# Inverse roots of two normalisations on one engine, and another order for the last step of the down projection

## The chip, the cores and the metric

The kernel runs on one core of a Trainium2 chip. The core has five engines, each with a queue of instructions that it works through in order: TensorE (PE, matrix products, its weight loads shown as PEld), VectorE (DVE), ScalarE (ACT), GpSimd (POOL) and SyncE (SP), which here only issues transfers. Transfers run on 16 DMA engines beside them. Engines wait for each other on semaphores. The metric is the time of one execution on the device in microseconds (us), the median of several runs.

## The reference

One block of a sequence model for 1024 positions of 1024 channels, in float32. What matters here is the second half: the attention output is projected and added to the residual, normalised, and a gated feed-forward layer follows; a last normalisation makes the output.

```python
def rmsnorm(x, g):
    xf = x.astype(jnp.float32)
    xf = xf * lax.rsqrt(jnp.mean(xf * xf, axis=-1, keepdims=True) + RMS_EPS)
    return (xf * g.astype(jnp.float32)).astype(x.dtype)
...
        merged = (jax.nn.sigmoid(gate_a) * y_a + jax.nn.sigmoid(gate_b) * y_b) @ w_o[l]
        x = x + g1 * merged

        h = modulate(rmsnorm(x, norm2_g[l]), sh2, sc2)
        ffn = (jax.nn.silu(h @ w_ffn_gate[l]) * (h @ w_ffn_up[l])) @ w_ffn_down[l]
        x = x + g2 * ffn
    return rmsnorm(x, norm_f_g)
```

## The kernel before, in words

Positions are cut into eight row blocks of 128 (t = 0 to 7), channels into halves of 512. Every matrix product in float32 precision is made of three products of split operands: a high part h (a cast on ScalarE), a low part l (the rest, a subtraction on VectorE), and the pairs (h,h), (h,l), (l,h). A scheduler moves instructions of the program within each engine's queue; the order that it chose is what the rows further down show.

**Attention output** (`attend_out`, lines 1112 to 1178). For every row block two PSUM tiles of 128x512 are made and added to x (line 1141). ScalarE squares the row and sums it (line 1150); `rstd` (lines 479 to 497) turns the sum into an inverse root; ScalarE multiplies (line 1152), TensorE transposes (line 1160), and the scaled transposes are the operands of the feed-forward layer.

`rstd` works on 128x1: VectorE scales and adds epsilon (line 485, and 487 where two half sums come), ScalarE takes Ln (488) and Exp(-0.5 x) (489), and VectorE corrects that by one Newton step: a = y v y (491), a = 1.5 - 0.5 a (495), y = y a (496).

**Down projection** (`down`, lines 1280 to 1412). It is a product of 1024 x 2816 by 2816 x 1024 after Strassen's scheme: blocks of half the rows by half the channels, and seven products (numbered 1 to 7) in place of eight. The 20 pairs of channels blocks that go this way are done in three steps of 4, 3 and 3 (`STEPS`); two last blocks come afterwards in plain form (`rest`). In each step the products run in `ORDER` = 2, 4, 5, 3, 1, 6, 7. For a product, sums of weight blocks are made on POOL (line 1339), cast on ScalarE (1340), the low part taken on VectorE (1341); then four PSUM tiles t of 128x512, each of 9 matmuls in a step of three (line 1356), are added by VectorE to that product's own accumulator `acc[i]` (line 1362). An accumulator is two buffers, each with two of the four tiles.

Four of the accumulators (4, 5, 7, 6) also hold the residual of their block and gather the result. What Strassen's scheme adds between them is done by POOL in the last step (`closing`, line 1317, table `CLOSE`): for each n, the position of a product in the step, a list of (target, source, operation), four tiles each. `closing(n)` stands in the program ahead of the matmul tiles of position n, and `closing(7)` behind the step.

PSUM has eight banks of 128x512, named gu (1), wo (3) and tq (4). `self.banks` hands them out in turn. Each product takes four, so a product has the banks of the one two positions ahead of it.

**Tail** (lines 1380 to 1412). For each row block in the order 4, 5, 6, 7, 0, 1, 2, 3 (`ROWS`) two tiles of six matmuls give the rest of the sum (line 1396). VectorE adds the gathered block (1398); ScalarE squares (1406; for the last row in halves, 1400); `close` calls `rstd`, multiplies by the root and the gain (1381; last row 1375 on ScalarE for the left half and 1376 on VectorE for the right) and sends the row out (1378, 1382). Rows 4 to 7 read accumulators 2 and 6, rows 0 to 3 accumulators 7 and 5.

Of the kernel before, what the change touches and what calls it, by code (L numbers as in the profile page):

```python
# [9 lines left out]
F32 = mybir.dt.float32  # L10
# [18 lines left out]
class S5:  # L29
# [270 lines left out]
    def run(self, m, u_src, y_dst, more):  # L300
# [56 lines left out]
        if more:  # L357
# [30 lines left out]
SIGN_A = {i: ALU.subtract if i in (6, 7) else ALU.add for i in range(1, 8)}  # L388
SIGN_B = {i: ALU.subtract if i in (3, 4) else ALU.add for i in range(1, 8)}

CLOSE = {2: ((6, 2, ALU.subtract),), 3: ((2, 4, ALU.add),), 4: ((7, 4, ALU.add),), 5: ((7, 5, ALU.subtract), (5, 3, ALU.add)),
         6: ((6, 3, ALU.add), (6, 1, ALU.add)), 7: ((7, 1, ALU.add),)}
SLOT = {3: 0, 6: 1, 7: 2, 4: 3, 1: 4, 2: 5, 5: 6}

AENG = {(i, 1) for i in range(1, 8)} | {(2, 0)}
# [32 lines left out]
class Block:  # L428
# [47 lines left out]
        (lo or nc.vector).tensor_tensor(l, a, h.bitcast(F32), ALU.subtract)  # L476
        return h, l

    def rstd(self, pool, ss, n, more=None, at=None):

        nc = self.nc
        v = at("v") if at else pool.tile([P, n], F32, name="rv")
        y = at("y") if at else pool.tile([P, n], F32, name="ry")
        a = at("a") if at else pool.tile([P, n], F32, name="ra")
        nc.vector.tensor_scalar(v, ss if more is None else more, 1.0 / 1024.0, 1e-6, ALU.mult, ALU.add)
        if more is not None:
            nc.vector.scalar_tensor_tensor(v, ss, 1.0 / 1024.0, v, ALU.mult, ALU.add)
        self.after(nc.scalar.activation(y, v, AF.Ln), self.fence)
        nc.scalar.activation(y, y, AF.Exp, scale=-0.5)
        if n == 1:  # L490
            nc.vector.scalar_tensor_tensor(a, y, v, y, ALU.mult, ALU.mult)
        else:
            nc.vector.tensor_tensor(a, y, y, ALU.mult)
            nc.vector.tensor_tensor(a, a, v, ALU.mult)
        nc.vector.tensor_scalar(a, a, -0.5, 1.5, ALU.mult, ALU.add)
        nc.vector.tensor_tensor(y, y, a, ALU.mult)
        return y

    def after(self, ins, first):
# [617 lines left out]
    def attend_out(self, mg, g1, const, tp, pp, tpp):  # L1117
# [5 lines left out]
        for c in range(2):  # L1123
# [7 lines left out]
            for t in range(KT):  # L1131
                if c or t > 3:
                    ps[t] = pp.tile([P, 512], F32, name="wo")
                    self.wo_product(ps[t], t, range(KT), mg, ws)
                elif t == 0:
                    for tt in range(4):
                        ps[tt] = tpp.tile([P, 512], F32, name="tq")
                    for k in range(KT):
                        for tt in range(4):
                            self.wo_product(ps[tt], tt, (k,), mg, ws)  # L1140
                nc.vector.tensor_tensor(x1[t][:, cs], ps[t], x1[t][:, cs], ALU.add)
                if c == 0:
                    continue
                nc.sync.dma_start(out=self.xD[P * t:P * t + P], in_=x1[t])
                if t % 4 == 0:
                    f = [[self.F.tile([P, 2, 512], F32, name=f"f{y}") for _ in range(2)] for y in range(2)]
                xh = self.rp.tile([P, 1024], F32, name="row") if t % 4 == 3 else tp.tile([P, 1024], F32, name="xh")
                xhs.append(xh)
                ss = const.tile([P, 1], F32, name="ss2", bufs=2)
                nc.scalar.activation(xh, x1[t], AF.Square, accum_out=ss)  # L1150
                r = self.rstd(const, ss, 1)
                nc.scalar.mul(xh, x1[t], r)
                if t % 2 == 0:
                    continue
                for k in range(0, KT, 2):
                    q = tpp.tile([P, 512], F32, name="tq").rearrange("p (k t) -> p k t", k=2)
                    s = slice(P * (t % 4 - 1), P * (t % 4 - 1) + 256)
                    for kk in range(2):
                        for tt in range(2):
                            nc.tensor.transpose(q[:, kk, P * tt:P * tt + P], xhs[t - 1 + tt][:, P * (k + kk):P * (k + kk) + P], self.ident)  # L1160
                        o = f[k // 4][k % 4 // 2][:, kk, s]
                        G_, m_ = G[:, k + kk:k + kk + 1], mod[:, k + kk:k + kk + 1]
                        if kk:
                            nc.vector.tensor_scalar(o, q[:, kk], G_, m_, ALU.mult, ALU.add)  # L1164
                        else:
                            nc.scalar.activation(o, q[:, kk], AF.Identity, bias=m_, scale=G_)
                if t == 3:
                    b11, b21 = f
                    self.B = {2: self.pieces(2, b11, None, self.PA, "pa"), 4: self.pieces(4, b21, b11, self.PA, "pa")}
# [111 lines left out]
    def down(self, const, tp, g2, gf):  # L1281
# [38 lines left out]
        last_sum = None  # L1320
        stages = Turns(*[(self.W, "wb", 4)] * 4, *self.stages.pools)
        for s, np_ in enumerate(STEPS):
            W = [(weights(2 * p), weights(2 * p + 1)) for p in range(p0, p0 + np_)]
            if s == len(STEPS) - 1:
                WL = [weights(20 + m) for m in range(2)]
            for n, i in enumerate(ORDER):
                ops = []
                (ay, ax), b = TERMS_B[i]
                for p in range(np_):
# [10 lines left out]
                        nc.scalar.copy(h, st)  # L1340
                        nc.vector.tensor_tensor(l, st, h.bitcast(F32), ALU.subtract)
                    ops.append((h, l))
                if s == len(STEPS) - 1:
                    if n == 6:
                        rest = []
                        for m in range(2):
# [4 lines left out]
                for t in range(4):  # L1351
# [7 lines left out]
                    if s == 0 and i not in FROM:  # L1359
                        (nc.scalar.copy if (n * 4 + t) % 2 else nc.vector.tensor_copy)(m[i], ps)  # L1360
                    else:
                        nc.vector.tensor_tensor(m[i], ps, m[i], ALU.add)
            p0 += np_
        closing(7)
        ops = rest
        out = self.out.rearrange("o (t p) d -> p (o t) d", p=P)
        L, R = slice(0, 512), slice(512, 1024)

        def at(t):
            return lambda n: small[:, t, "vya".index(n) + 2:"vya".index(n) + 3]  # L1370

        def close(t, row, ss):
            if t == ROWS[-1]:
                r = self.rstd(const, ss[:, 1:2], 1, ss[:, 0:1], at(t))
                nc.scalar.mul(row[:, L], row[:, L], r)
                nc.vector.scalar_tensor_tensor(row[:, R], row[:, R], r, gf[:, R], ALU.mult, ALU.mult)
                for cs in (L, R):
                    nc.sync.dma_start(out=out[:, t, cs], in_=row[:, cs])
                return
            r = self.rstd(const, ss[:, 0:1], 1, None, at(t))  # L1380
            nc.vector.scalar_tensor_tensor(row, row, r, gf, ALU.mult, ALU.mult)
            nc.sync.dma_start(out=out[:, t], in_=row)

        small = const.tile([P, KT, 5], F32, name="ss3")
        last = None
        for t in ROWS:
            ss = small[:, t, 0:2]
# [2 lines left out]
            for c in range(2):  # L1390
# [8 lines left out]
                if t == ROWS[-1]:  # L1399
                    nc.scalar.activation(sq[:, cs], row[:, cs], AF.Square, accum_out=ss[:, c:c + 1])  # L1400
                    if c == 0:
                        nc.gpsimd.tensor_tensor(row[:, cs], row[:, cs], gf[:, cs], ALU.mult)
                if c == 0 and last:
                    close(*last)
# [136 lines left out]
```

## Time and profile before

| What | Value |
|---|---|
| runs | 1508.24, 1510.94, 1508.77 us |
| median | 1508.77 us |
| the profiled execution's own time | 1510.83 us |
| its span | 1509.1 us |
| mean granted TensorE clock | 0.974 |
| HBM read, written | 142.40 MB, 48.76 MB |

The span goes from the first to the last instruction of the execution that was profiled, and its own time is a little longer than the span. Times in the trace are microseconds from the span's start. Names are the program's: `tq`, `wo`, `gu` are PSUM banks, `pb` and `x1` (shown as `x` by the profile) the buffers of the accumulators, `pa` the rows of weights and of the output, `ss` the small sums. "out<-in" gives what is written and what is read; a name in square brackets behind a row is the instruction that ended the idle time before it.

In the last stage the span divides so: step 2's products end near 1410, the last step runs to about 1468, the rest rows to 1493, and behind them no matmul stands.

### The profile page before, as it was taken

What the parts mean: (1) busy time and instruction counts of PE and PEld (TensorE: products, weight loads), DVE (VectorE), ACT (ScalarE), POOL (GpSimd) and SP (SyncE); (2) the same over time, 40 slices, a digit from 0 to 9 for tenths busy, and PEclk for the clock granted to TensorE, in tenths of its full rate; (3) what the DMA queues carried; (4) which work ended last, traced back from release to release, by engine and by line L of the source; (5) the groups of instructions that cost most, each with busy time, mean ns of one, the idle gap of its engine ahead of it and who ended that gap; (6) DMA issues with size and microseconds to landing.
All of it is one profiled execution on the core that took longest, in us unless ns stands there. A gap on an engine that the chain in (4) does not pass through costs nothing.

```text
span 1509.1 us, 18300 instructions
## 1 busy us (share of the span) xinstructions
PE 1421.0 (94%) x6706; PEld 1121.5 (74%) x6706; DVE 1137.7 (75%) x1523; ACT 582.8 (39%) x764; POOL 610.9 (40%) x306
## 2 busy tenths in 40 slices
PE   5898999999999999999799799999999998999995
PEld 3678888787666666668688588888888886888774
DVE  5879995457897888868526886666666669999997
ACT  3321122722565655663226533333333334433323
POOL 1000000102555555414300235444444468788795
PEclk9999999999999999999899899999999999999998
DMA  9555665489011112136422233333333346455312
GB/s 341 136 108 165 165 159 150 130 272 328 15 49 49 37 34 77 56 104 217 175 84 106 76 125 113 105 105 105 106 105 105 104 154 235 136 161 176 102 49 112
DMA packets 180410, 193.55 MB, mean 128 GB/s; under 512 B 28636, under 2 KB 130080, under 8 KB 180320
## 3 DMA queue, kind: packets, MB, share of 16 engines
q1 hardware_dynamic: 171184, 184.86, 38.9%
q10 hardware_dynamic: 8912, 7.48, 1.8%
q8 instruction: 53, 0.87, 0.2%
q14 instruction: 37, 0.30, 0.1%
q0 software_dynamic: 224, 0.05, 0.0%
HBM read 142.40 MB, written 48.76 MB: 127 GB/s over the span
## 4 chain that ended last, share of the span: by engine, by line
PE 51%; DVE 20%; issue 10%; POOL 9%; DMA 5%; ACT 4%; SPq 1%; DVEq 0%; POOLq 0%; ACTq 0%
PE tq L1257 10%; PE wo L1257 8%; PE ga L735 4%; PE wo L1114 4%; PE mm L735 3%; PE mm L809 3%; PE gu L1257 3%; PE mx L809 3%; POOL ws L874 3%; PE mm L643 2%; PE mx L735 2%; PE tq L1114 2%; PE acc L809 1%; POOL pb L1317 1%; PE z L809 1%
## 5 line engine op out<-in xcount | busy, mean ns | idle before, releaser
L874 POOL TENSOR_SCALAR ws<-wa 128x1024 f32<-128x1024 f32 (+1 forms) x40 | 108.5, 2712 | 112.9 <-DVE wa L871 59.2
L473 POOL TENSOR_TENSOR ws<-wb 128x1024 f32<-128x1024 f32 x26 | 64.2, 2471 | 193.8 <-DVE f L1164 90.9
L457 POOL TENSOR_TENSOR wl<-ws,wh 128x1024 fp32r<-128x1024 f32 x12 | 28.9, 2410 | 127.0 <-ACT wh L454 127.0
L294 POOL MEMSET tz<- 128x1024 f32 x4 | 3.8, 954 | 178.0 <-PE mm L643 95.9
L877 DVE TENSOR_TENSOR ws<-wa,ws 128x1024 f32<-128x1024 f32 (+1 forms) x40 | 46.6, 1165 | 35.5 <-ACT ws L876 35.1
L875 ACT ACTIVATE ws<-ws 128x1024 f32<-128x1024 f32 (+1 forms) x40 | 38.8, 971 | 74.7 <-POOL ws L874 74.7
L1310 POOL TENSOR_TENSOR pa<-pa,row 128x1024 f32<-128x1024 f32 x22 | 64.7, 2965 | 1.8 <-DMA pa<-in_w_ffn_down_dram 1.6
L473 POOL TENSOR_TENSOR wgs<-wb 128x1024 f32<-128x1024 f32 x14 | 34.6, 2473 | 72.3 <-DVE wgl L476 30.9
L1248 POOL TENSOR_TENSOR f<-f,f 128x512 f32<-128x512 f32 x30 | 50.0, 1692 | 26.9 <-DVE f L1238 18.3
L879 DVE TENSOR_TENSOR wl<-ws,wh 128x1024 fp32r<-128x1024 f32 (+1 forms) x40 | 55.2, 1381 | 1.1
L902 DVE TENSOR_TENSOR wa<-wa,acc 128x512 f32<-128x512 f32 (+1 forms) x80 | 46.7, 623 | 2.1 <-PE acc L809 1.8
L454 ACT CAST wh<-ws 128x1024 fp32r<-128x1024 f32 x24 | 25.1, 1048 | 59.9 <-PE wo L1114 36.3
L979 DVE SCALAR_TENSOR_TENSOR acc<-aw,cond,acc 128x512 f32<-128x512 f32 x56 | 43.8, 781 | 5.9 <-DMA aw<-in_w_ada_dram 5.1
L1237 ACT ACTIVATE f<-f 128x1024 f32<-128x1024 f32 x22 | 23.4, 1061 | 62.7 <-DVE f L1277 32.8
L1339 POOL TENSOR_TENSOR wb<-pa 128x512 f32<-128x512 f32 x23 | 40.6, 1776 | 15.6 <-DVE wxl L1337 5.5
L809 PE MATMUL z<-q,k 64*128 64x512 f32 (+3 forms) x192 | 41.8, 526 | 3.8 <-DVE wa L871 2.6
L1248 POOL TENSOR_TENSOR f<-f 128x512 f32<-128x512 f32 x20 | 42.2, 2129 | 0.0
L905 ACT ACTIVATE wa<-wa 128x1024 f32<-128x1024 f32 (+1 forms) x40 | 38.5, 963 | 9.0 <-DVE wa L902 9.0
L1356 PE MATMUL wo<-f,f 128*128 128x512 f32 x132 | 40.6, 389 | 0.0
L809 PE MATMUL mm<-wa,V 128*64 128x512 f32 (+3 forms) x192 | 39.8, 507 | 0.0
L900 ACT CAST row<-acc 1x1024 fp32r<-1x1024 f32 (+2 forms) x32 | 27.0, 842 | 31.2 <-PE acc L809 31.0
L876 ACT ACTIVATE ws<-ws 128x1024 f32<-128x1024 f32 (+1 forms) x40 | 38.6, 966 | 0.5
(844 smaller groups left out, 4725.0 us busy)
## 6 DMA issues: line engine op xcount, KB each, us to landing
aw<-in_w_ada_dram SPq DMA_DIRECT2D x64, 256.0 KB, 4.4
hD<-f SPq DMA_DIRECT2D x30, 512.0 KB, 2.9
ws<-in_w_in_dram SPq DMA_DIRECT2D x23, 512.0 KB, 4.6
wb<-in_w_ffn_gate_dram SPq DMA_DIRECT2D x44, 256.0 KB, 4.1
wb<-in_w_ffn_up_dram SPq DMA_DIRECT2D x44, 256.0 KB, 4.3
pa<-in_w_ffn_down_dram SPq DMA_DIRECT2D x22, 512.0 KB, 4.6
wb<-hD SPq DMA_DIRECT2D x40, 256.0 KB, 2.8
x<-in_x_dram SPq DMA_DIRECT2D x16, 512.0 KB, 6.9
```

Source lines behind the costliest of these rows:

```text
L473: (add or nc.gpsimd).tensor_tensor(st, a, b, op)
L735: self.nc.tensor.matmul(ps, lhsT=w[a][:, k], rhs=act[h][k][:, b], start=(j == 0), stop=(j == n - 1))
L809: return self.tc.keep_in_program_order(self.nc.tensor.matmul(*args, **kw))
L874: nc.gpsimd.tensor_scalar(st, a, EXACT, None, ALU.min)
L877: nc.vector.tensor_tensor(st, a, st, ALU.max)
L879: nc.vector.tensor_tensor(lt, st, ht.bitcast(F32), ALU.subtract)
L902: nc.vector.tensor_tensor(a[:, x, 0:f], a[:, x, 0:f], r[:, x, 0:f], ALU.subtract)
L979: nc.vector.scalar_tensor_tensor(acc, w[:, j], cj, acc, ALU.mult, ALU.add)
L1114: self.nc.tensor.matmul(ps, lhsT=mg[t // 4][k][:, a, P * (t % 4):P * (t % 4) + P], rhs=ws[k // 2][b][:, k % 2], start=k + j == 0, stop=k + ...
L1248: nc.gpsimd.tensor_tensor(o, a, b, op)
L1257: self.nc.tensor.matmul(ps, lhsT=w[x][:, q, k], rhs=self.B[i](y, k), start=(j == 0), stop=(j == 11))
L1310: nc.gpsimd.tensor_tensor(w, w, g2, ALU.mult)
```

## The change

Three things are changed.

1. `rstd` keeps its old form for another place only. At the attention output and at the end, `rstd_s` takes its place: six operations on ScalarE. With s the sum of squares: y = exp(-0.5 ln(s/1024 + eps)), h = -0.5 (s/1024 + eps), h = h y, h = h y + 1.5, y = y h. Epsilon and 1.5 come from a small buffer `eps` that POOL fills with three stores at the start. For the last row, two more operations of ScalarE turn the first half's sum into the addends for the second half's.

2. In the last step the products run in the order 5, 2, 4, 1, 3, 6, 7 (`LAST`), and `CLOSE` is rewritten for it; nothing is closed behind the step.

3. In the last step products 3 and 1 are no longer added to their own accumulators but to the two blocks that they belong to each (`DIRECT`): 3 to blocks 5 and 6, 1 to blocks 6 and 7. The parts of products 3 and 1 from the earlier steps still come through POOL's closings. There are 32 closing additions of 128x512 before and after, and eight more additions of VectorE after.

```diff
-CLOSE = {2: ((6, 2, ALU.subtract),), 3: ((2, 4, ALU.add),), 4: ((7, 4, ALU.add),), 5: ((7, 5, ALU.subtract), (5, 3, ALU.add)),
-         6: ((6, 3, ALU.add), (6, 1, ALU.add)), 7: ((7, 1, ALU.add),)}
+LAST = (5, 2, 4, 1, 3, 6, 7)
+CLOSE = {1: ((7, 5, ALU.subtract),), 2: ((5, 3, ALU.add), (6, 3, ALU.add)), 3: ((6, 2, ALU.subtract), (6, 1, ALU.add)),
+         4: ((7, 1, ALU.add), (2, 4, ALU.add)), 5: ((7, 4, ALU.add),)}
+DIRECT = {3: (5, 6), 1: (6, 7)}
...
+    def rstd_s(self, ss, y, h, b=None):
+
+        act = self.nc.scalar.activation
+        b, bh = b or (self.eps[:, 0:1], self.eps[:, 1:2])
+        self.after(act(y, ss, AF.Ln, bias=b, scale=1.0 / 1024.0), self.fence)
+        act(y, y, AF.Exp, scale=-0.5)
+        act(h, ss, AF.Identity, bias=bh, scale=-0.5 / 1024.0)
+        self.nc.scalar.mul(h, h, y)
+        act(h, h, AF.Identity, bias=self.eps[:, 2:3], scale=y)
+        self.nc.scalar.mul(y, y, h)
         return y
...
+        self.eps = const.tile([P, 3], F32, name="eps")
+        for n, x in enumerate((1e-6, -0.5e-6, 1.5)):
+            nc.gpsimd.memset(self.eps[:, n:n + 1], x)
...
-                r = self.rstd(const, ss, 1)
+                r = self.rstd_s(ss, *(const.tile([P, 1], F32, name=n, bufs=2) for n in ("r2", "h2")))
...
+            final = s == len(STEPS) - 1
...
-            for n, i in enumerate(ORDER):
+            for n, i in enumerate(LAST if final else ORDER):
...
-                        nc.vector.tensor_tensor(m[i], ps, m[i], ALU.add)
+                        for z in DIRECT.get(i, (i,)) if final else (i,):
+                            nc.vector.tensor_tensor(m[z], ps, m[z], ALU.add)
             p0 += np_
-        closing(7)
...
             if t == ROWS[-1]:
-                r = self.rstd(const, ss[:, 1:2], 1, ss[:, 0:1], at(t))
+                r = self.rstd_s(ss[:, 1:2], small[:, t, 2:3], small[:, t, 3:4], (small[:, t, 4:5], small[:, t, 5:6]))
...
-            r = self.rstd(const, ss[:, 0:1], 1, None, at(t))
+            r = self.rstd_s(ss[:, 0:1], small[:, t, 2:3], small[:, t, 3:4])
...
                     if c == 0:
+                        for n, f in ((4, 1.0), (5, -0.5)):
+                            nc.scalar.activation(small[:, t, n:n + 1], ss[:, 0:1], AF.Identity, bias=self.eps[:, n - 4:n - 3], scale=f / 1024.0)
                         nc.gpsimd.tensor_tensor(row[:, cs], row[:, cs], gf[:, cs], ALU.mult)
```

Behind the lines of the diff the queues of the engines look as follows at three places. Lines of the changed kernel are some ten higher than those of before: its closings are line 1327, VectorE's adds from PSUM 1374, the low parts 1352, the weight sums 1350.

POOL in the last step, before. The buffers are the accumulators: pb_9843/44 is 4, pb_9847/48 is 5, pb_9851/52 is 7, x1_9855/56 is 2, x1_9857/58 is 3, x1_9859/60 is 1 and x1_9861/62 is 6.

```order
L1317 TENSOR_TENSOR pb_9851<-pb_9851,pb_9847 128x512 x2
L1317 TENSOR_TENSOR pb_9852<-pb_9852,pb_9848 128x512 x2
L1317 TENSOR_TENSOR pb_9847<-pb_9847,x1_9857 128x512 x2
L1317 TENSOR_TENSOR pb_9848<-pb_9848,x1_9858 128x512 x2
L1317 TENSOR_TENSOR x1_9861<-x1_9861,x1_9857 128x512 x2
L1317 TENSOR_TENSOR x1_9861<-x1_9861,x1_9859 128x512
L1317 TENSOR_TENSOR x1_9862<-x1_9862,x1_9858 128x512
L1317 TENSOR_TENSOR x1_9861<-x1_9861,x1_9859 128x512
L1317 TENSOR_TENSOR x1_9862<-x1_9862,x1_9858 128x512
L1317 TENSOR_TENSOR x1_9862<-x1_9862,x1_9860 128x512
L1317 TENSOR_TENSOR pb_9851<-pb_9851,x1_9859 128x512
L1317 TENSOR_TENSOR x1_9862<-x1_9862,x1_9860 128x512
```

POOL in the last step of the change. Here 4 is pb_9839/40, 5 is pb_9843/44, 7 is pb_9847/48, 2 is x1_9851/52, 3 is x1_9853/54, 1 is x1_9855/56 and 6 is x1_9857/58.

```order
L1327 TENSOR_TENSOR pb_9844<-pb_9844,x1_9854 128x512
L1327 TENSOR_TENSOR x1_9858<-x1_9858,x1_9852 128x512
L1350 TENSOR_TENSOR ws_11424<-pa_10967 128x512
L1327 TENSOR_TENSOR x1_9858<-x1_9858,x1_9852 128x512
L1350 TENSOR_TENSOR ws_11431<-pa_10973 128x512
L1327 TENSOR_TENSOR x1_9857<-x1_9857,x1_9855 128x512
L1350 TENSOR_TENSOR wgs_11438<-pa_10979 128x512
L1327 TENSOR_TENSOR x1_9857<-x1_9857,x1_9855 128x512
L1327 TENSOR_TENSOR x1_9851<-x1_9851,pb_9839 128x512 x2
L1327 TENSOR_TENSOR x1_9858<-x1_9858,x1_9856 128x512
L1327 TENSOR_TENSOR x1_9852<-x1_9852,pb_9840 128x512
L1327 TENSOR_TENSOR x1_9858<-x1_9858,x1_9856 128x512
```

Before, the additions to block 6 are among POOL's last work of the step. In the change they stand between weight sums (line 1350) for the last two products, and the last row here is the 31st from the first addition to block 6 in this step, `x1_9857<-x1_9857,x1_9853`.

VectorE at products 3 and 1 of the last step, before: each tile goes to its own accumulator.

```order
L1341 TENSOR_TENSOR wl_11345<-wb_11342,wh_11344 128x1024
L1362 TENSOR_TENSOR x1_9857<-gu_11222,x1_9857 128x512
L1362 TENSOR_TENSOR x1_9857<-wo_11233,x1_9857 128x512
L1362 TENSOR_TENSOR x1_9858<-wo_11244,x1_9858 128x512
L1341 TENSOR_TENSOR wgl_11352<-wb_11349,wgh_11351 128x1024
L1362 TENSOR_TENSOR x1_9858<-wo_11255,x1_9858 128x512
L1341 TENSOR_TENSOR wxl_11411<-ws_11408,wxh_11410 128x1024
L1341 TENSOR_TENSOR f0_11418<-ws_11415,f0_11417 128x1024
L1362 TENSOR_TENSOR x1_9859<-tq_11291,x1_9859 128x512
L1362 TENSOR_TENSOR x1_9859<-tq_11302,x1_9859 128x512
L1362 TENSOR_TENSOR x1_9860<-tq_11313,x1_9860 128x512
L1341 TENSOR_TENSOR f0_11425<-wgs_11422,f0_11424 128x1024
```

VectorE at products 1 and 3 of the change.

```order
L1374 TENSOR_TENSOR pb_9847<-gu_11230,pb_9847 128x512
L1374 TENSOR_TENSOR x1_9857<-wo_11242,x1_9857 128x512
L1374 TENSOR_TENSOR pb_9847<-wo_11242,pb_9847 128x512
L1352 TENSOR_TENSOR wgl_11372<-wb_11369,wgh_11371 128x1024
L1352 TENSOR_TENSOR wxl_11427<-ws_11424,wxh_11426 128x1024
L1352 TENSOR_TENSOR f0_11434<-ws_11431,f0_11433 128x1024
L1374 TENSOR_TENSOR pb_9843<-tq_11307,pb_9843 128x512
L1374 TENSOR_TENSOR x1_9857<-tq_11307,x1_9857 128x512
L1374 TENSOR_TENSOR x1_9858<-wo_11254,x1_9858 128x512
L1374 TENSOR_TENSOR pb_9848<-wo_11254,pb_9848 128x512
L1374 TENSOR_TENSOR pb_9843<-tq_11319,pb_9843 128x512
L1374 TENSOR_TENSOR x1_9857<-tq_11319,x1_9857 128x512
```

Tiles of the banks wo and tq now go to block 6 (x1_9857/58) and to another block each, and the low parts for products 6 and 7 (line 1352) stand between them in the queue.

ScalarE at the very end, before: the two half squares of the last row, and Ln and Exp of the last two rows.

```order
L1400 ACTIVATE ft_11688,ss3_11505<-pa_11687 128x512
L488 ACTIVATE ss3_11505<-ss3_11505 128x1
L1400 ACTIVATE ft_11688,ss3_11505<-pa_11687 128x512
L489 ACTIVATE ss3_11505<-ss3_11505 128x1
L488 ACTIVATE ss3_11505<-ss3_11505 128x1
L489 ACTIVATE ss3_11505<-ss3_11505 128x1
L1375 ACTIVATE pa_11687<-pa_11687,ss3_11505 128x512
```

ScalarE at the very end of the change, from the last half square on.

```order
L1408 ACTIVATE ft_11692,ss3_11509<-pa_11691 128x512
L499 ACTIVATE ss3_11509<-ss3_11509 128x1
L498 ACTIVATE ss3_11509<-ss3_11509 128x1
L500 ACTIVATE ss3_11509<-ss3_11509 128x1
L501 ACTIVATE ss3_11509<-ss3_11509 128x1
L499 ACTIVATE ss3_11509<-ss3_11509 128x1
L502 ACTIVATE ss3_11509<-ss3_11509,eps_91 128x1
L501 ACTIVATE ss3_11509<-ss3_11509 128x1
L503 ACTIVATE ss3_11509<-ss3_11509 128x1
L502 ACTIVATE ss3_11509<-ss3_11509,eps_91 128x1
L503 ACTIVATE ss3_11509<-ss3_11509 128x1
L1383 ACTIVATE pa_11691<-pa_11691,ss3_11509 128x512
```

Ten operations of 128x1 now stand between the last half square and the product; no other engine works between them.

More of the change, by code (lines that the diff above doesn't have):

```diff
@@ L477, in operand, with rstd @@
         return h, l
-    def rstd(self, pool, ss, n, more=None, at=None):
+    def rstd(self, pool, ss, n):
         nc = self.nc
[L482 to L487, printed above, removed]
+        v, y, a = (pool.tile([P, n], F32, name=x) for x in ("rv", "ry", "ra"))
+        nc.vector.tensor_scalar(v, ss, 1.0 / 1024.0, 1e-6, ALU.mult, ALU.add)
         self.after(nc.scalar.activation(y, v, AF.Ln), self.fence)
         nc.scalar.activation(y, y, AF.Exp, scale=-0.5)
[L490 to L494, printed above, removed]
+        nc.vector.tensor_tensor(a, y, y, ALU.mult)
+        nc.vector.tensor_tensor(a, a, v, ALU.mult)
         nc.vector.tensor_scalar(a, a, -0.5, 1.5, ALU.mult, ALU.add)
         nc.vector.tensor_tensor(y, y, a, ALU.mult)
+        return y
+    def rstd_s(self, ss, y, h, b=None):
[7 more added lines that the diff above has]
+        self.nc.scalar.mul(y, y, h)
         return y
@@ L1322, in down @@
         for s, np_ in enumerate(STEPS):
+            final = s == len(STEPS) - 1
             W = [(weights(2 * p), weights(2 * p + 1)) for p in range(p0, p0 + np_)]
-            if s == len(STEPS) - 1:
+            if final:
                 WL = [weights(20 + m) for m in range(2)]
-            for n, i in enumerate(ORDER):
+            for n, i in enumerate(LAST if final else ORDER):
                 ops = []
@@ L1342, in down @@
                     ops.append((h, l))
-                if s == len(STEPS) - 1:
+                if final:
                     if n == 6:
@@ L1367, in down @@
         L, R = slice(0, 512), slice(512, 1024)
-        def at(t):
-            return lambda n: small[:, t, "vya".index(n) + 2:"vya".index(n) + 3]
         def close(t, row, ss):
             if t == ROWS[-1]:
-                r = self.rstd(const, ss[:, 1:2], 1, ss[:, 0:1], at(t))
+                r = self.rstd_s(ss[:, 1:2], small[:, t, 2:3], small[:, t, 3:4], (small[:, t, 4:5], small[:, t, 5:6]))
                 nc.scalar.mul(row[:, L], row[:, L], r)
@@ L1379, in close @@
                 return
-            r = self.rstd(const, ss[:, 0:1], 1, None, at(t))
+            r = self.rstd_s(ss[:, 0:1], small[:, t, 2:3], small[:, t, 3:4])
             nc.vector.scalar_tensor_tensor(row, row, r, gf, ALU.mult, ALU.mult)
             nc.sync.dma_start(out=out[:, t], in_=row)
-        small = const.tile([P, KT, 5], F32, name="ss3")
+        small = const.tile([P, KT, 6], F32, name="ss3")
         last = None
```

## The prediction

> **What bounds the kernel now.** I read the busy shares first, then the chain of work that ended last, then the stretches in which the change lies, and in those the waits and the timeline.
>
> ```profile
> PE 1421.0 (94%) x6706; PEld 1121.5 (74%) x6706; DVE 1137.7 (75%) x1523; ACT 582.8 (39%) x764; POOL 610.9 (40%) x306
> PE 51%; DVE 20%; issue 10%; POOL 9%; DMA 5%; ACT 4%; SPq 1%; DVEq 0%; POOLq 0%; ACTq 0%
> 1420.00:1440.00 20.00, 20.00 (x90) 16.57 (x89) 20.00 (x19) 6.39 (x7) 19.37 (x11) 1.00 0.34 93
> 1440.00:1460.00 20.00, 20.00 (x90) 16.57 (x89) 16.49 (x18) 6.38 (x7) 20.00 (x12) 1.00 0.20 66
> 1460.00:1480.00 20.00, 17.38 (x76) 13.75 (x75) 17.00 (x20) 3.53 (x7) 20.00 (x13) 1.00 0.00 1
> 1493.00:1509.00 16.00, 0.00 (x0) 0.00 (x0) 11.67 (x29) 5.82 (x17) 1.26 (x1) 0.66 0.50 197
> ```
>
> TensorE (PE) is busy 94% of the 1509.1 us, so work on another engine is worth something only where PE waits for it. The average hides that the last stage differs: in the table of stretches (busy time of PE, PEld, DVE, ACT, POOL, then clock, DMA share, GB/s) POOL is full from 1420 to 1480, the last product step, while PE is full too up to 1460. From 1493 PE has nothing left, and 16 us pass on DVE, ACT and the last transfer. The change touches three places: the attention output (about 825 to 850), the last product step, and that tail. Times below stand on the clock of the profiled execution before: 1510.83 us, of which the span is 1509.1; it lies 2.06 over the median 1508.77.
>
> **Attention output: six ScalarE operations in place of two ScalarE and four VectorE ones, eight rows.**
>
> ```profile
> PE tq L1160 <- ACT xh L1152: 2.5, 1, 2.5
> PE tq L1160 <- ACT row L1152: 1.6, 1, 1.6
> PE tq L1257 <- ACT x L475: 3.6, 1, 3.6
> 825.28 0.20 ACT L1150 ACTIVATION_READ_ACCUMULATOR xh<-x 128x1 f32 x1
> 833.66 1.22 DVE L476 TENSOR_TENSOR x<-ws,x 128x1024 fp32r<-128x1024 f32 x1
> 834.80 0.21 DVE L491 SCALAR_TENSOR_TENSOR ra<-ry,rv 128x1 f32<-128x1 f32 x1
> 838.46 0.15 DVE L496 TENSOR_TENSOR ry<-ry,ra 128x1 f32<-128x1 f32 x1
> 838.64 1.15 ACT L1152 ACTIVATE xh<-x,ry 128x1024 f32<-128x1024 f32 x1 [1.40 <-DVE ry L496]
> 840.93 1.15 ACT L1152 ACTIVATE row<-x,ry 128x1024 f32<-128x1024 f32 x1 [0.67 <-DVE ry L496]
> ```
>
> The sum of squares of row 6 is there at 825.5, its product only at 838.64: the small steps stand between VectorE splits of 1.2 us each. On ScalarE alone they need about 1.7 us (0.2 to 0.3 each, priced at the tail below), so row 6 is ready before PE asks. PE's waits of 2.5 and 1.6 us can go: 4.1 at most. Late next are VectorE's splits behind the transposes; the later wait of 3.6 us for a cast stays. I take -3.5, with bounds 0 (the splits set that end anyway) and -6 (4.1, and some 2 us of VectorE's queue less).
>
> **Last step, the terms that pull up.** The number of POOL closings is 32 before and after, and PE's matmuls are the same. What is new: products 3 and 1 are added out of PSUM to two blocks each, eight more VectorE adds (0.6 us each, in time that VectorE's 65 small operations give back), and the adds of product 1 to block 6 come, by the data, behind POOL's closings of that block with 3, 2 and 1. That is a new wait. VectorE works in order: behind a waiting add stand the other adds that free PSUM banks and the splits for products 6 and 7. PE then waits, since the seven products take their banks in turns and product 6 needs those of product 1.
>
> ```profile
> 1407.09 1.88 DVE L1362 TENSOR_TENSOR x<-tq,x 128x512 f32<-128x512 f32 x3
> L1317 POOL TENSOR_TENSOR x<-x,x 128x512 f32<-128x512 f32 x12 | 18.6, 1572 | 0.0
> L1317 POOL TENSOR_TENSOR pb<-pb 128x512 f32<-128x512 f32 x8 | 17.1, 2151 | 0.0
> L1317 POOL TENSOR_TENSOR pb<-pb,x 128x512 f32<-128x512 f32 x8 | 14.0, 1780 | 0.0
> L1317 POOL TENSOR_TENSOR x<-x,pb 128x512 f32<-128x512 f32 x4 | 8.1, 2030 | 0.0
> L1339 POOL TENSOR_TENSOR wb<-pa 128x512 f32<-128x512 f32 x4 | 7.1, 1789 | 0.6 <-DVE wl L1337 0.6
> L1339 POOL TENSOR_TENSOR ws<-pa 128x512 f32<-128x512 f32 x2 | 2.6, 1292 | 0.0
> L1339 POOL TENSOR_TENSOR wgs<-pa 128x512 f32<-128x512 f32 x1 | 1.3, 1293 | 0.0
> 1451.25 0.39 PE L1356 MATMUL gu<-wh 128*128 128x512 f32 x1
> 1457.37 0.39 PE L1356 MATMUL wo<-wh 128*128 128x512 f32 x1
> 1456.72 8.00 POOL L1317 TENSOR_TENSOR pb<-pb 128x512 f32<-128x512 f32 x4
> 1472.60 8.80 POOL L1317 TENSOR_TENSOR x<-x,x 128x512 f32<-128x512 f32 x7
> 1471.42 2.47 DVE L1362 TENSOR_TENSOR pb<-tq,pb 128x512 f32<-128x512 f32 x4
> ```
>
> The first of these closings can start when VectorE has added the first tile of step 2's product 6 to the block: 1407.09 + 0.68 = 1407.8. From there to the one that product 1's fourth tile waits for, POOL has 35 instructions in the new order (31 rows, four of them double), all of 128x512. The seven groups of 1421.6 to 1489.7 give their price there: 39 in 18.6 + 17.1 + 14.0 + 8.1 + 7.1 + 2.6 + 1.3 = 68.8 us busy, in 68.0 us of wall time since neighbours overlap a little: 1.743 each. So 35 x 1.743 = 61.0, ready at 1468.8. Two adds and the handoff make 1.3: the bank is free at 1470.1. Product 6 starts in the trace at 1451.25, and its fourth tile, the one that takes that bank, at 1457.37. PE waits 1470.1 - 1457.4 = **+12.7 us**. Ends: at 1.26 each, the price of the seven from 1472.60, the closings are done at 1451.8 and the wait is nothing; at 2.15, the dearest group, at 1483.1, which makes 27; I widen that to +31 for three queued splits of 1.2 us. I take 12.7, the mean price in this very step. The trace's 1472.60 run lies beside VectorE adds that read one operand from PSUM, the 2.00 each from 1456.72 beside splits.
>
> The Trainium skill, "SBUF — State Buffer", section "Who interferes with whom", says that a VectorE instruction with two SBUF inputs holds the read port that GpSimd needs for its whole length, and that one with at most one SBUF input does not contend. The trace agrees, 1.26 against 2.00 us. By this rule a VectorE that waits would let POOL through faster; with 20 operations at 1.74 and then 15 at 1.26 the wait would be 5.4 us and the sum 7.3 lower; this is the third rival below.
>
> I hold to the mean, since after an add VectorE's queue has a split next, as the order rows show.
>
> **What a stall costs besides.**
>
> ```profile
> 863.96 5.91 PE tq L1257 x13
> 860.00:870.00 10.00, 6.54 (x15) 4.96 (x16) 10.00 (x8) 5.44 (x7) 3.24 (x1) 0.66 0.03 7
> ```
>
> After PE's idle of 3.6 us there, 13 matmuls took 5.91 us where the same take 0.227 each (27 of them from 1451.25 to 1457.37 above), 2.95 in all: +2.96, at a granted clock of 0.66 over the stretch. A wait of 12.7 us in one piece brings that too: **+3.0**, once; it is 0 if the wait breaks into short pieces, 6 if it comes twice.
>
> The Trainium skill, "TensorE: Matmul & The Clock Gate", Part 1, says that an idle window of about 3.4 us halves the clock until about 3.4 us of work have gone by. The trace agrees with 3.6 us idle and the 5.91; by that rule the four waits of product 6, were they below 3.4 us each, would cost no more than themselves, and the sum would be 3.0 lower.
>
> **Tail.**
>
> ```profile
> 1492.32 0.39 PE L1396 MATMUL tq<-wh,wl 128*128 128x512 f32 x1
> 1498.49 0.68 DVE L1398 TENSOR_TENSOR pa<-tq,pb 128x512 f32<-128x512 f32 x1
> 1499.20 0.63 ACT L1400 ACTIVATE ft<-pa 128x512 f32<-128x512 f32 x1
> 1499.73 0.19 ACT L1400 ACTIVATION_READ_ACCUMULATOR ft<-pa 128x1 f32 x1
> 1478.76 0.20 ACT L489 ACTIVATE ss<-ss 128x1 f32<-128x1 f32 x1
> 1480.39 1.03 DVE L496 TENSOR_TENSOR ss<-ss 128x1 f32<-128x1 f32 x1
> L1406 ACT ACTIVATE ft<-pa 128x1024 f32<-128x1024 f32 x7 | 7.4, 1060 | 19.9 <-DVE pa L1398 19.9
> 1504.15 0.72 ACT L1375 ACTIVATE pa<-pa,ss 128x512 f32<-128x512 f32 x1 [1.80 <-DVE ss L496]
> 1504.90 0.82 SPq L1378 DMA_DIRECT2D out_dram<-pa  x2
> ```
>
> Before: the last matmul ends at 1492.7, the span at 1509.1, 16.4 us. VectorE is behind: small steps stretched up to 1.03 us stand between its adds. After: add 0.68, half square 0.63 + 0.19, ten small operations of ScalarE, product 0.72, and 1509.1 - 1504.90 = 4.2 for the transfer. A small one costs 0.20 by the row at 1478.76; some now read a second operand by pointer, which the full-row product shows to cost 0.1 (1.15 against 1.06), so 0.3 and 3.0 for ten: 9.4 in all, -7.0. ScalarE's share of a row is 1.06 + 0.19 + 6 x 0.27 = 2.87, PE's twelve matmuls 2.72, so it falls up to 1 us behind in seven rows; half of it counts. **-6.5.** Bounds: -8 at 0.20 each; at 0.72 each, the half-row product as the dearest, -3.
>
> The scheduler also swaps a few PE and ScalarE instructions near 190 to 300 us. There PE waits once:
>
> ```profile
> PE ga L735 <- ACT yp L1013: 2.3, 1, 2.3
> ```
>
> I take 0, bounds -2 and +2.
>
> **Sum.** -3.5 + 12.7 + 3.0 - 6.5 + 0 = +5.7: the profiled execution would go from 1510.83 to 1516.5, and the median from 1508.77 to **1514.5 us**.
>
> **Rivals.**
>
> *Faster: POOL is through in time.* Under 1.385 us per operation ((1457.4 - 1.3 - 1407.8) / 35 = 1.38) PE does not wait at all. Then -3.5 - 6.5 is left, with about 1 us for short waits: 1499.8. For it: PSUM adds leave POOL at 1.26. Against it: the groups above, of which only the three for ws and wgs have a mean under 1.385. 0.22.
>
>
>
> *Slower, and deeper than my forecast:* the splits for products 6 and 7, queued on VectorE behind the blocked adds, come after the bank is free; PE then waits for four of them (1.2 us each) beyond the 12.7, and the clock falls twice: -3.5 + 17.5 + 6 - 6.5 = +13.5, 1522.3. It decides when more than two splits stand behind the last blocked add. 0.2.
>
> *Within 0.2%* (3 us, about what a measurement of this kernel can tell from no change): POOL runs 20 operations at 1.74 and, while VectorE stands at its wait, 15 at 1.26, so the bank is free at 1462.8 and the wait is 5.4: -3.5 + 5.4 + 3.0 - 6.5 = -1.6, 1507.2. For it: the run from 1472.60. Against it: VectorE has splits between the blocked adds. 0.15. My forecast itself, one long wait at product 6, has 0.43.
>
> *Not what it says:* the data order could let VectorE's adds of product 1 go ahead of POOL's closings; but both write block 6 and the closings stand first in the program. It would give the first rival's 1499.8, and is in its chance.
>
> **How the numbers follow.** Slower 0.43 + 0.2 = 0.63, same 0.15, faster 0.22. The likeliest case's own range is 1510 to 1520. The range for 8 in 10 takes in the first rival and the deeper loss: 1499 to 1523; the extreme bounds, +31 at the step among them, stay outside.
>
> **What would show it.** In the changed profile: waits of PE for VectorE at the banks gu and wo near 1455 to 1475, of 9 to 15 us in all, with VectorE in turn waiting for POOL at line 1374; a slice of half clock there; PE's waits at the transposes of the attention output below 1 us; 9 to 10.5 us from the last matmul to the end. I am wrong if POOL's operations from 1408 on take under 1.4 us, if the bank waits are small, or if the tail keeps more than 12 us.

## The result, and the profile after

The changed kernel takes 1526.28 us in the median of four runs (1520.44 to 1531.80), beside 1509.53 for the kernel before: a ratio of 1.012, 95% interval 1.0077 to 1.0163. It is slower, as forecast, but by some 17 us in place of 6, outside the range of 1499 to 1523. Measured again with another five runs it took 1522.88 (1521.31 to 1524.93) beside 1509.11: 1.0098, 1.0078 to 1.0118. The profiled execution took 1522.29 us, with a span of 1520.5.

The busy shares of the changed kernel, from its page:

```profile
PE 1430.9 (94%) x6706; PEld 1121.9 (74%) x6706; DVE 1132.9 (75%) x1466; ACT 600.7 (40%) x830; POOL 612.4 (40%) x309
```

As many matmuls take 10 us longer. The stretches that answer to those of before (time, then busy PE, PEld, DVE, ACT, POOL, the clock, DMA share, GB/s):

```profile
1420.00:1440.00 20.00, 19.39 (x86) 15.56 (x85) 20.00 (x22) 6.95 (x7) 18.13 (x11) 1.00 0.36 94
1440.00:1460.00 20.00, 15.67 (x69) 12.55 (x67) 11.27 (x9) 4.31 (x5) 20.00 (x14) 0.95 0.30 92
1460.00:1480.00 20.00, 14.25 (x37) 10.46 (x38) 17.72 (x21) 5.35 (x6) 20.00 (x14) 0.62 0.00 0
1480.00:1500.00 20.00, 20.00 (x88) 16.07 (x87) 18.24 (x21) 7.57 (x23) 7.93 (x4) 1.00 0.07 27
1511.00:1520.50 9.50, 0.00 (x0) 0.00 (x0) 4.40 (x4) 4.16 (x18) 1.26 (x1) 0.59 0.42 166
```

PE is no longer full from 1440 to 1480; from 1460 to 1480 the trace shows 37 matmuls where it had 90 in a full stretch, at a clock of 0.62. POOL is full there, as it was before. VectorE, which was busy for 16.5 us of the stretch from 1440, is busy for 11.3. What PE waits for there, with the sum, the number and the longest of the waits; and then rows of the timeline of VectorE, POOL and PE, with the idle time ahead and what ended it in brackets:

```profile
PE gu L1367 <- DVE pb L1374: 6.9, 1, 6.9
PE wo L1367 <- DVE pb L1374: 1.9, 1, 1.9
PE gu L1367 <- DVE wgl L1352: 1.3, 1, 1.3
```

```profile
1447.36 3.94 DVE L1352 TENSOR_TENSOR wl<-wb,wh 128x1024 fp32r<-128x1024 f32 x2
1461.11 0.69 DVE L1374 TENSOR_TENSOR x<-gu,x 128x512 f32<-128x512 f32 x1 [9.80 <-POOL x L1327]
1461.72 0.68 DVE L1374 TENSOR_TENSOR pb<-gu,pb 128x512 f32<-128x512 f32 x1
1463.57 0.69 DVE L1374 TENSOR_TENSOR x<-wo,x 128x512 f32<-128x512 f32 x1 [1.17 <-POOL x L1327]
...
1464.77 2.33 DVE L1352 TENSOR_TENSOR wgl<-wb,wgh 128x1024 fp32r<-128x1024 f32 x1
1411.27 4.69 POOL L1327 TENSOR_TENSOR x<-x,x 128x512 f32<-128x512 f32 x3
...
1470.42 2.25 POOL L1327 TENSOR_TENSOR x<-x,x 128x512 f32<-128x512 f32 x1
1462.54 0.77 PE L1367 MATMUL gu<-wh 128*128 128x512 f32 x1 [6.88 <-DVE pb L1374]
```

The new wait is there: VectorE stands 9.8 us at the add of bank gu to block 6, until POOL has closed that tile, and PE stands 6.9 us at bank gu, for the first tile of product 6 already. Behind the adds come three splits (the low parts of operands: wgl at 1464.77, then wxl and f, to 1471.5), and only behind them the adds that free the bank of the third tile; PE waits for them again.

From here on I compare kernels by stage. The first column is the time of the first matmul of the attention output (line 1114 of before); then come the stretches to the first transpose (1160), from there to the first matmul of the down products (1356), to the first of the rest rows (1396), to the end of the last matmul, and to the end of the span:

| kernel | start | output | transposes, gate and up | three steps | rest | tail | span |
|---|---|---|---|---|---|---|---|
| before | 730.7 | 61.0 | 473.0 | 203.4 | 24.6 | 16.4 | 1509.1 |
| after | 732.1 | 62.1 | 472.8 | 221.0 | 22.7 | 9.8 | 1520.5 |

The steps are 17.6 longer, rest and tail together 8.5 shorter. But at the attention output, where PE's waits at the transposes have fallen to 0.3 us (the later wait for a cast has grown from 3.6 to 4.8), nothing was won in the third column, and 2.5 us more have passed ahead of it.

### The profile page after: what moved, and what is told of

Read it like the earlier page. It is cut to its first block, busy times and chain, and to the rows that moved or that the text cites. A ratio compares the mean times of both kernels' runs of the same rounds, so it can differ in the third digit from the quotient of the medians.

```text
span 1520.5 us, 18297 instructions
## 1 busy us (share of the span) xinstructions
PE 1430.9 (94%) x6706; PEld 1121.9 (74%) x6706; DVE 1132.9 (75%) x1466; ACT 600.7 (40%) x830; POOL 612.4 (40%) x309
## 4 chain that ended last, share of the span: by engine, by line
PE 55%; DVE 20%; issue 8%; DMA 6%; POOL 6%; ACT 4%; SPq 0%; DVEq 0%; POOLq 0%; ACTq 0%
PE tq L1267 10%; PE wo L1267 9%; PE wo L1124 4%; PE ga L745 4%; PE tq L1367 3%; PE gu L1267 3%; PE mm L819 3%; PE mx L819 3%; POOL ws L884 3%; PE mm L653 2%; DMA aw<-in_w_ada_dram 2%; PE tq L1124 2%; PE wo L1367 2%; PE acc L819 2%; PE mm L745 2%
## 5 line engine op out<-in xcount | busy, mean ns | idle before, releaser
L885 ACT ACTIVATE ws<-ws 128x1024 f32<-128x1024 f32 (+1 forms) x40 | 38.9, 972 | 73.8 <-POOL ws L884 73.8
L456 ACT CAST wh<-ws 128x1024 fp32r<-128x1024 f32 x24 | 25.1, 1048 | 62.1 <-PE wo L1124 36.6
L478 DVE TENSOR_TENSOR wl<-ws,wh 128x1024 fp32r<-128x1024 f32 x20 | 28.5, 1425 | 15.5 <-ACT wh L477 15.3
```

## The experiments

**The parts by themselves.** Four kernels: before with the new order, closings and double adds alone; with the six operations at the final normalisation alone; at the attention output alone; and at both.

The first, order_only, has these lines of the change, with `CLOSE` and `DIRECT` as there:

```diff
+LAST = (5, 2, 4, 1, 3, 6, 7)
...
+            for n, i in enumerate(LAST if final else ORDER):
...
+                        for z in DIRECT.get(i, (i,)) if final else (i,):
+                            nc.vector.tensor_tensor(m[z], ps, m[z], ALU.add)
             p0 += np_
-        closing(7)
```

The second, tail_only, has the buffer `eps` and these; attend_only has the buffer and the other line; roots_only has both.

```diff
-            r = self.rstd(const, ss[:, 0:1], 1, None, at(t))
+            r = self.rstd_s(ss[:, 0:1], small[:, t, 2:3], small[:, t, 3:4])
```

```diff
-                r = self.rstd(const, ss, 1)
+                r = self.rstd_s(ss, *(const.tile([P, 1], F32, name=n, bufs=2) for n in ("r2", "h2")))
```

> Before, with the new order of the last step, its closings and the double adds alone; the roots stay in their old form on two engines. Theory: the whole loss is here. Two terms were read in the profile after, 10.1 us of PE waits at products 6 and 7 and 5.4 us of half clock, and 2 us more in the steps ahead: 16 to 19 us slower than before, and the PE waits for VectorE's adds at gu stand in the trace. Rival: VectorE's old chain of small operations keeps it behind anyway, so part of the loss is hidden in the tail: 8 to 12 us slower.

> Before, with the six operations on ScalarE at the final normalisation alone. Theory: the tail after the last matmul goes from 16.4 to about 9.5 us and the rows ahead gain 1 to 2: 6 to 9 us faster. Rival: in the undelayed step VectorE is late from the closings of POOL, not from the small operations, so it gains 3 us or less.

> Before, with the six operations on ScalarE at the attention output alone. Theory from the profile after: PE no longer waits at the transposes (4.1 us), but the wait for a cast of the feed-forward operands grows and the section is no shorter: within 1.5 us of before. Rival, as forecast: 3.5 us faster, and the section was lost to something else in the changed kernel.

> Before, with the six operations on ScalarE at both places and the old order of the last step. If the parts add up: the sum of the two runs that have one place each, 5 to 9 us faster than before. If the early shift of 1.4 us that the profile after shows ahead of the attention output comes with the constants' stores, it is in this trace too, and the gain is 1.4 smaller than the sum.

| kernel | start | output | transposes, gate and up | three steps | rest | tail | median | ratio (95%) |
|---|---|---|---|---|---|---|---|---|
| order_only | 733.6 | 60.8 | 473.1 | 221.9 | 21.9 | 11.1 | 1522.67 | 1.0087 (1.0060 to 1.0114) |
| tail_only | 735.6 | 60.4 | 479.0 | 203.4 | 26.6 | 11.9 | 1517.59 | 1.0050 (1.0031 to 1.0069) |
| attend_only | 731.4 | 61.8 | 476.9 | 203.2 | 26.4 | 14.4 | 1517.26 | 1.0044 (1.0020 to 1.0068) |
| roots_only | 731.2 | 60.7 | 473.7 | 203.5 | 25.1 | 13.5 | 1510.57 | 1.0006 (0.9993 to 1.0020) |

The kernel before took 1509.13 beside them. None of the four came out as expected. The order alone is 13.5 us slower, between the two figures. It brings the loss in the steps, 18.5 us, but also 8.0 of the 8.5 us that rest and tail gain, with the roots in their old form. Each place of the roots alone makes the kernel 8 us slower, and both together cost nothing: parts that don't add up. The losses lie in stages that the edit doesn't touch: with the final roots alone, the gate and up products take 6.0 us more.

In that stage PE is busy without a break in every kernel, so I counted matmuls. The stretch 900 to 1200 of before, of the changed kernel and of the one with the roots at both places, in this order:

```profile
900.00:1200.00 300.00, 300.00 (x1325) 248.41 (x1324) 191.89 (x211) 94.03 (x106) 150.53 (x73) 1.00 0.33 105
```

```profile
900.00:1200.00 300.00, 300.00 (x1313) 246.21 (x1312) 190.07 (x209) 92.65 (x103) 147.81 (x70) 1.00 0.32 102
```

```profile
900.00:1200.00 300.00, 300.00 (x1313) 246.34 (x1312) 190.00 (x209) 91.50 (x103) 147.53 (x71) 1.00 0.31 101
```

PE is at 300.00 of 300 and at full clock in all, and yet it does 12 matmuls fewer in two of them. The mean distance of two starts of the gate and up matmuls there (the pitch) is 227.4 ns before and with the order alone, 229.4 in the changed kernel and with both roots, 230.4 and 231.2 with one place each. What the slow ones have in common is not an instruction but the small buffer for epsilon and what else is new among the constants: it moves the buffers pa and pb and the weights wh, wl and wgh by 64 to 192 bytes per partition, while x1, f0, wb and wxh, placed from the other end, stay.

**Only the addresses.** An unused buffer of 64 bytes per partition in the kernel before; and the same in the changed kernel and in the one with both roots, which makes their shift 256 bytes in place of 192.

```diff
+        self.pad = const.tile([P, 16], F32, name="pad")
+        nc.gpsimd.memset(self.pad, 0.0)
         self.ident = const.tile([P, P], F32, name="ident")
```

> Before, with nothing but an unused buffer of 64 bytes per partition among the constants, so that the buffers behind it lie 64 bytes further while those placed from the other end stay. Theory (addresses): the matmul pitch of the feed-forward stage goes from 227.4 ns to 229 to 231 as in the four kernels with the roots on ScalarE, by operand pair, and the kernel is 5 to 9 us slower, like the run with the final roots alone. Rival (order): the pitch comes from what the other engines do beside the matmuls; then the pitch stays 227 and the time is that of before within 2 us.

> After, with 64 bytes more among the constants, so that the shift against before is 256 bytes in place of 192. Theory (addresses, with a period of 256 bytes or a divisor of it): the pitch returns to 227.4 ns and the time falls by 4 to 9 us, to that of the run with the order alone less 1 to 3 us. Rival: the pitch stays at 229 to 230 and so does the time (within 2 us of after).

> Before with the six operations on ScalarE at both places, the old order of the last step, and the shift of 256 bytes in all. Theory: with the pitch back at 227.4 ns it is 4 to 8 us faster than the run without the 64 bytes (1510.6) and the fastest of all, 1503 to 1506. Rival: the pitch stays and so does the time, 1510 to 1511.

| kernel | shift | start | output | transposes, gate and up | three steps | rest | tail | median | ratio (95%) |
|---|---|---|---|---|---|---|---|---|---|
| before_pad64 | 64 | 733.5 | 61.0 | 477.5 | 203.2 | 26.5 | 14.5 | 1517.92 | 1.0051 (1.0032 to 1.0070) |
| after_pad | 256 | 732.6 | 60.0 | 468.7 | 224.6 | 22.6 | 9.9 | 1519.22 | 1.0067 (1.0049 to 1.0086) |
| roots_pad | 256 | 734.7 | 61.5 | 469.4 | 203.3 | 24.6 | 13.9 | 1506.80 | 0.9975 (0.9962 to 0.9989) |

The kernel before took 1510.93 beside them. Sixty-four unused bytes cost 7 us; in the profile 4.5 of them lie in the stage from the transposes on. The same matmuls of one tile, moving buffer x1 with the weights wh, from the timeline of before and then of the padded one:

```profile
1018.97 0.62 PE L1257 MATMUL gu<-x,wh 128*128 128x512 f32 x2
...
1021.69 0.62 PE L1257 MATMUL wo<-x,wh 128*128 128x512 f32 x2
```

```profile
1022.93 0.63 PE L1259 MATMUL gu<-x,wh 128*128 128x512 f32 x2
...
1025.73 0.63 PE L1259 MATMUL wo<-x,wh 128*128 128x512 f32 x2
```

Between the two rows lie the twelve matmuls of one tile: 2.72 us before, 2.80 padded, 227 against 233 ns each. It goes by pairs of operands: in the padded kernel x1 with wgh takes 233.3 (226.5 before) and pb with wxh 230.4 (226.5), while pb with wh (226.6) and pb with wgh (226.7) are untouched. The slow pairs have one operand in the shifted buffers and one in those that stay; pairs of one side take 226.6 to 228.3. At 192 bytes, in the changed kernel, pb with wxh takes 233.3 and x1 with wgh 229.1. With 256 bytes all are back at 226.5, and the distance is 227.4 in the mean. So the pitch depends on how two operands of a matmul lie to each other: slow at shifts of 64, 160 and 192 bytes, quick at 0 and 256. The stage from the transposes to the down products then gives 473.0 to 469.4 or 468.7: the 3.6 to 4.3 us that the attention output was to bring.

The padded changed kernel has the instructions of the changed one in the same order, and yet its steps are 3.6 us longer. A row of VectorE's timeline, one of PE's waits and a row of POOL's timeline, all of the padded kernel:

```profile
1458.91 9.63 DVE L1354 TENSOR_TENSOR wgl<-wb,wgh 128x1024 fp32r<-128x1024 f32 x1
PE gu L1369 <- DVE wgl L1354: 8.6, 1, 8.6
1464.99 2.47 POOL L1329 TENSOR_TENSOR pb<-pb,x 128x512 f32<-128x512 f32 x2
```

The split that took 2.33 us in the changed kernel, beside POOL operations of 2.25, takes 9.63 here. POOL's operations run on beside it at 1.25 each to 1467.46, and the split ends 1.1 us after that, at 1468.54. In no other trace of this document does an operation of VectorE take more than 3.5 us. Why VectorE and POOL went in turn in one execution, and POOL alone for seven operations in another, is not shown.

**What VectorE waits for.** The padded after with the closings of block 6 first and those of block 7 last.

```diff
+CLOSE = {0: ((6, 3, ALU.add), (6, 1, ALU.add)), 2: ((6, 2, ALU.subtract),), 4: ((7, 5, ALU.subtract), (5, 3, ALU.add)),
+         5: ((2, 4, ALU.add), (7, 1, ALU.add), (7, 4, ALU.add))}
```

> After with the same 64 bytes, and with the closings in another order: block 6 gets the old parts of products 3 and 1 at the head of the last step, and the subtraction of product 2 next, while the closings of 7 come later; the number of POOL's additions and of VectorE's is the same. Theory: the wait of product 6 for product 1's banks (6.9 us in the profile after) falls under 2 us; product 3's adds to block 5 now come behind some 31 of POOL's operations, 54 us, so product 7 waits instead, some 4 to 7 us: 3 to 8 us faster than the padded after. Rival: the closings are not what VectorE waits for, and the wait at product 6 stays at 6 to 8 us.

It took 1517.24 us (1.0049, 1.0031 to 1.0067), 2 us less than the padded after, with 220.1 us for the steps (224.6 there, the long split among them, and 221.0 in the changed kernel). PE's waits in it, behind the start of the last step:

```profile
PE tq L1369 <- DVE x L1376: 5.8, 2, 3.9
PE tq L1369 <- DVE f L1354: 2.6, 1, 2.6
...
PE gu L1369 <- DVE wgl L1354: 0.2, 1, 0.2
```

The wait at bank gu for the double adds is gone, and the wait has moved to bank tq, where product 7 needs what product 3 holds: 8.4 us. VectorE does wait for the closings; the gain is less than the 3 to 8 expected, and the 8.4 us that moved are more than the 4 to 7 expected.

**Order or double adds.** The same order of products, but every product to its own accumulator, and all of 3 and 1 closed by POOL; still 32 closings.

```diff
+CLOSE = {1: ((7, 5, ALU.subtract),), 2: ((6, 2, ALU.subtract),), 3: ((2, 4, ALU.add),), 4: ((7, 4, ALU.add),), 5: ((5, 3, ALU.add),),
+         6: ((6, 3, ALU.add), (6, 1, ALU.add)), 7: ((7, 1, ALU.add),)}
+DIRECT = {}
```

> The padded after with the same order of products in the last step, but each product added to its own accumulator alone, and all of products 3 and 1 brought in by POOL's closings as before the change: 32 additions of POOL, no double adds of VectorE. Theory: the new wait hangs on the double adds, not on the order 5, 2, 4, 1, 3: the last two steps and the first take 203 to 206 us from the first down matmul to the first rest matmul (224.6 in the padded after), and the time is that of the run with the roots and 256 bytes, 1505 to 1509. Rival: the order of the products costs by itself, and 8 us or more of the 21 stay.

The steps take 201.1 us, 23.5 less than in the padded after, 19.9 less than in the changed kernel and 2.2 less than in the old order; PE waits 0.2 us in the last of them. The loss hangs on the double adds with their closings, not on the order. Rest and tail are 24.3 and 16.9, so the whole is 1509.74 (1.0006, 0.9992 to 1.0021), just above what was expected: the tail's gain has gone with the stall.

**Why the tail is shorter.** Before, with POOL's last 12 closings left out (3 and 1 to block 6, 1 to block 7), and the old roots.

```diff
-         6: ((6, 3, ALU.add), (6, 1, ALU.add)), 7: ((7, 1, ALU.add),)}
+         }
...
-        closing(7)
```

> Before with 12 of the 32 closings left out: those of products 3 and 1 to block 6 and of product 1 to block 7, the last ones in the order. The roots stay in their old form. Theory: the tail is long since POOL's closings run beside it and stretch VectorE's operations; from the last matmul to the end it falls from 16.4 to about 11, the rest rows from 24.6 to about 22.5, and the time by 6 to 8 us. Rival, as the prediction had it: the small operations on VectorE make the tail long, and it stays above 14.

The tail goes from 16.4 to 11.1 with the small operations still on VectorE; the rest rows stay at 24.6, against expectation, and the time falls by 4.9 us (0.9969, 0.9956 to 0.9982), less than expected. At the end of before POOL still runs its closings to 1489.6, 3 us short of the last matmul; here is what follows, before and then without those 12, and then the one wait of VectorE for POOL in before from 1460 on, which is not there without them:

```profile
1480.00:1493.00 13.00, 12.70 (x57) 10.17 (x55) 12.90 (x25) 5.40 (x15) 9.62 (x7) 1.00 0.20 81
1493.00:1509.00 16.00, 0.00 (x0) 0.00 (x0) 11.67 (x29) 5.82 (x17) 1.26 (x1) 0.66 0.50 197
```

```profile
1493.00:1503.70 10.70, 0.00 (x0) 0.00 (x0) 6.25 (x16) 2.72 (x9) 1.26 (x1) 0.71 0.50 197
```

```profile
DVE pa L1398 <- POOL x L1317: 2.4, 2, 1.9
```

VectorE has 11.7 us of work left behind the last matmul, and 6.3 without. The closings hold it up in two ways: its adds of the rest rows wait 2.4 us for them, and its operations beside them are longer (the one at 1480.39, 1.03 us, takes 0.16 without them, the first product with root and gain 1.79 against 1.27). The changed kernel has its POOL done at 1487.9 and its last matmul at 1510.7: the stall gives POOL the time.

**The changed kernel again, and a smaller step.**

> The changed kernel itself once more, beside the runs of this call. Theory: with the pitch of 229.4 ns it is 4 to 9 us slower than the padded after (1519.2), 1523 to 1528, and some of its runs near 1530 as in the first four. Rival: the four first runs were high by chance, and it lies within 2 us of the padded after.

It took 1522.88, 3.7 us more than the padded one (13.8 above its own before, where the padded one is 8.3 above its own); its profile gives the stages of the first again (472.7, 221.1, 22.7, 9.8). Its five runs lie within 3.6 us; none of them reached the 1530 of two of the first four.

```diff
+LAST = (2, 4, 5, 3, 1, 6, 7)
+CLOSE = {0: ((6, 1, ALU.add), (7, 1, ALU.add)), 2: ((6, 2, ALU.subtract),), 5: ((2, 4, ALU.add), (7, 4, ALU.add), (7, 5, ALU.subtract)),
+         6: ((6, 3, ALU.add), (5, 3, ALU.add))}
+DIRECT = {1: (6, 7)}
```

> The roots on ScalarE and 256 bytes, the old order of the products, and only product 1 added to blocks 6 and 7 in the last step; its old part is closed first of all, product 2's next, the closings of 7 and of product 3 last. POOL has 32 closings still. Theory: some 19 of POOL's operations, 33 us from 1408, stand ahead of the double adds, so they are done by 1441, before product 1's tiles end; PE does not wait for them, and POOL, which starts its closings earlier, ends earlier, so that the tail is shorter: 1501 to 1505. Rival: VectorE's four more adds and the contention bring waits at products 6 and 7: 1507 or more.

The rival was right: 1511.73 (1.0021, 1.0007 to 1.0035), 209.8 us for the steps with waits for double adds (2.0) and splits (1.2), and a tail of 13.0. Of the kernels that leave nothing out, the quickest is the one with both roots, the old order and 256 bytes: 1506.80, a quarter of a per cent quicker than before.

## Why the prediction was right in its sign and wrong in its size

The sign, the place and the mechanism were right: VectorE's double adds behind POOL's closings, then PE behind VectorE at the banks gu and wo. All four signs that it named came: 10.1 us of waits at these banks, a slice of half clock, 0.3 us at the transposes, and 9.8 us behind the last matmul. By its steps:

- **POOL's 35 operations: 61.0 us forecast.** In the changed trace they run from 1411.27 to 1472.7, 61.4, with 2.6 of it idle. The price held although VectorE stood still for part of it: beside that wait they went at 1.26 each, elsewhere at up to 2.3.
- **The wait, +12.7, and half clock, +3.0.** Measured: 10.1 us (6.9, 1.3, 1.9) and about 4.3, from 22 matmuls at 0.43 us in place of 0.23; with the starts behind the waits the steps are 15.5 us longer from product 6 on, beside 15.7 forecast. That the sum fits so well is luck: the wait was too high and the half clock too low. I had worked out the fourth tile alone (at 1470.1; its bank came free at 1476.33, and it began at 1477.01). But the first tile's closing ended only at 1461.1, with PE ready at 1455.7, and its wait took the larger part; the last one, at 1473.99, is the third tile's, behind three splits. Ahead of product 6 another 2.1 us pass, with small waits for splits (0.9 and 0.6 the longest), which makes 17.6 for the steps.
- **Attention output, -3.5.** The mechanism is right: -3.6 and -4.3 where the buffers lie as before or 256 bytes off. In the changed kernel the stage from the transposes on shows -0.2. **This is where the prediction failed:** it priced every matmul that the change doesn't touch at its old duration, and had no term for addresses. Over the gate and up products that cost about 4 us, and all that the term was to bring; in the kernel before, 64 bytes cost 7. With 256 bytes the changed kernel lies 8.3 us above its own before, for 5.7 forecast.
- **Tail, -6.5.** Measured -8.5 with the rest rows, but for another reason. I put the lateness of VectorE down to its small operations. The roots alone bring -2.4 (roots_only, 25.1 + 13.5 against 41.0), the order alone -8.0, and leaving out late closings -5.3 in the tail. The ten operations of ScalarE cost 2.2 us, about 0.22 from start to start, for 3.0 forecast. That the tail came to 9.8 us for 9.4 forecast is luck in so far as POOL's part of it was not in the sum.
- **Early reorder, 0 within 2.** The first matmul of the attention output lies at 730.7 in before and between 731.2 and 735.6 in the other kernels, the one with 64 unused bytes (733.5) among them; 1.4 of the difference lies there. With the order alone it is 733.6, although that kernel has the instructions and addresses of before up to the last steps: executions alone differ by 2.9 there, so the 1.4 can't be put down to the change.

The deeper rival has a time, 1522.3, next to the measured ones, and its condition came true: three splits stand behind the last add that waits for POOL. But its price for the step, 17.5 + 6, is far above the 15.5 measured there, so the time agrees by luck.

The forecast +5.7 became +11.4 in the profile: about 4.4 from the attention term, 1.9 from the steps, 1.4 from the start, less 2.0 from the tail (5.7 in all). The median of the first four runs lies 17 above before, that of the second measurement 13.8; of the 2.4 between 11.4 and 13.8, 1.7 is that the profiled execution of before lies so far above the 1509.11. Two runs near 1530 in the first have no profile; a split held up for 9.63 us, as in the padded kernel, would be of that size, but whether they had one is open.

The rule of the Trainium skill, "SBUF — State Buffer", section "Who interferes with whom", that a VectorE instruction with two SBUF inputs contends with a GpSimd instruction that reads SBUF, held in its direction: POOL's eight operations from 1453.7 to 1463.5, while VectorE mostly waited, took 1.26 to 1.29 us each, against 2.25 beside splits. But over all 35 the mean was 1.74 as forecast, since those beside splits took up to 2.3.

## What to carry to other kernels

A buffer added anywhere ahead of the operands of matmuls can change the price of all of them: compare the count of matmuls in a stretch where PE is full before any stage is blamed, and pad the new buffer to a distance of the operands that was measured to be quick. An add that goes to a shared accumulator puts the owner of that accumulator in front of the PSUM bank; count the queue of that owner, in this case 35 operations, not the adds. A tail that is short because a stall ahead of it let another engine catch up is no gain: test the part alone.

## What the runs showed of the hardware

- Matmuls of 128x512 whose two operands lie in differently placed buffers take 227 ns or 229 to 235, by the distance of the buffers: quick at shifts of 0 and 256 bytes, slow at 64, 160 and 192. The clock column stays at 1.00 and PE is shown as full. Other distances were not tried, and what in the chip does it is not shown.
- After a wait of 6.9 us matmuls were issued every 0.43 us in place of 0.23, and the granted clock of the stretch was 0.62.
- After a further wait of 1.9 us, at 1473.99, came a second piece of slow matmuls from 1475.3 on, behind four at 0.23 to 0.27. The second profile of the changed kernel shows the same behind a wait of 2.1 us. What would come of such a wait without the first slow piece is not shown.
- A split of VectorE took 1.2 us by itself, 2.3 in turn with POOL operations of 2.25, and once 9.63 beside seven POOL operations of 1.25 that followed each other.
